# Moving the gates' chain of an mLSTM into the token-major part of a hybrid encoder block, the row product of x later, and neighbourhood operands a head at a time

## The chip, the cores and the metric

The kernel runs on one core of a Trainium2 chip. The core has five engines with queues of their own: TensorE (PE, matmuls and transposes; its weight loads are listed as PEld), VectorE (DVE), ScalarE (ACT), GpSimd (POOL) and SyncE (SP, which here only starts transfers). Each queue is worked off in its order; engines wait for each other by semaphores. The metric is the device time of one execution in microseconds, as the median of several runs.

## The reference

One block of an encoder over 512 tokens of width 1024, in float32. A normalised input is projected once, and three mixers read the projection: a bidirectional mLSTM, a neighbourhood attention on an 8 x 64 grid, and a cross-attention to 256 memory tokens. Cut to what matters here:

```python
h = rms_norm(x, mix_norm_g[l])
proj = h @ w_in[l]      # ml q,k,v,o | ml gates (16) | na q,k,v | xa q | merge gates
# mLSTM, per direction and head, from the gates i_pre, f_pre:
log_f = log_sigmoid(f_pre);  a = cumsum(log_f)
m_new = max(g_c + m, mw_c)                       # a running maximum: a scan
P = exp(D - m_j) * qk;  num = P @ v + inter_w * (C_prev @ q)
# neighbourhood attention, 8 heads of 64:
s = q @ k_band * NA_HEAD_DIM ** -0.5 + bias;  p = softmax(s);  o = p @ v_band
merged = g_ml*(y_ml @ w_br_ml) + g_na*(y_na @ w_br_na) + g_xa*(y_xa @ w_br_xa)
x = x + merged @ w_out
x = x + conv_glu_ffn(rms_norm(x))
return rms_norm(x)
```

## The kernel before, in words

Every big product is float32 accuracy out of three passes: weights and activations are split in a high and a low part, and `mm3` (lines 207 to 209) adds high x high, low x high and high x low in one PSUM bank. Weights come from memory in blocks of 128 x 1024 values or so, three blocks ahead (`emit_raw`, L155, on SP). Each block is split in two halves by `emit_split`: ACT copies the high half (L189, into four rotating buffers `wh`), DVE subtracts to get the low half (L190, `wl`).

The order of the stages on TensorE: four blocks of mLSTM q (`mlq`), four of k (`mlk`), then the *token-major part*, in which tokens lie on the partitions: three groups `c` = 0, 1, 2. Group 0 gives the 16 gates per token and half of the mLSTM's v, group 1 the other half and half of the neighbourhood's v, group 2 the rest. Group `c` is worked in weight blocks `h`; in group 1 there are four blocks of two k tiles, and each block runs over four token tiles `t`, 6 matmuls for each. Then come the other projections (`xaq`, `o`, `memk`, `memv`, `naq`, `nak`), the three branches with their gates (`g` and `br`), the output projection and the feed-forward part.

The attention-like parts are generators, advanced by `step` a few pieces after each block of a projection, so that their small products lie between the large ones. `ml_all` is the mLSTM, `xa_all` the cross-attention, `na_all` the neighbourhood attention; a branch's products wait until its generator is drained. Fewer pieces in one generator let the next start earlier. The code gives the order of emission; a scheduler may still exchange neighbouring instructions on an engine's queue.

What the change touches:

- The normalisation of x as a row (`rstd_row`). POOL raises the mean squares to the power -1/2 (L305); ACT and DVE split the result in two parts (L312, L313); DVE writes eight diagonal 128 x 128 tiles (L318); TensorE multiplies them with ones (L319, two products of 128 x 512) and ACT copies the row `rb` out of PSUM (L321). `proj` calls it inside the second `mlk` block, after k step 0 of 8. All convolutions on q and k (`conv`, L410 to L414, then `silu2`, L419 and L420) need `rb`. Their first instruction empties the PSUM bank that a later block uses again: four banks `mm`, four banks `at`.
- The gates' chain (`ml_prep`, L499 to L588). From the gates `Gt` DVE computes the logarithm of a sigmoid as a series (L503 to L524, with one exponential on ACT, L507) and copies it into `lfc` (L530, L531). Four transposes (L534) turn it into rows; ACT copies them (L536); DVE runs four scans over 512 tokens, two for the running maxima (L540, L541) and two for the sums (L551, L552); ACT copies (L553). DVE subtracts (L558) and POOL stores the result `rd` to memory (L560). Four transposes bring maxima and sums back into columns (L565); ACT takes exponentials and copies (L569, L570). `spread`, hung into the next projection by `late`, sends block sums to all partitions by one product (L573) and computes the decay weights `wt` and `dec` (L575 to L586). `ml_prep` is the first part of `ml_all`, advanced between the blocks of `xaq`.
- After it, per head: SP loads `rd` as rows on all partitions (`load_R`, L600), DVE adds masks (L608), ACT takes exponentials `E` (L660, L664), DVE multiplies them (L665, L667), and TensorE uses them (L675, L677).
- `na_all`. Two heads share 128 partitions. `prep(hp)` writes split operands for both heads of a pair: for each head ACT copies q, k and q again (L759 to L761, 64 x 512) and DVE makes two differences (L762, L763). It runs for the first pair at the start and then after each fourth of the 16 score steps. Each step does scores (L783, L784), a softmax (L788 to L796), transposes a step later (L802, split into `w` at L809, L810) and values two steps later (L821, stored by L833 to L842). The four operand tiles rotate under the tag `R`; bias tiles (L770) rotate under `nab`, a tag that two buffers of the gates' chain share.

Of the kernel before, what the change touches and what calls it, by code (L numbers as in the profile page):

```python
# [11 lines left out]
F32 = mybir.dt.float32  # L12
F32R = mybir.dt.float32r
# [4 lines left out]
P = 128  # L18
# [88 lines left out]
def hybrid_block(ctx, tc, xg, xT, memT, wflat, vecs, gbias, nabias, outa, outb):  # L107
# [14 lines left out]
    def nm(s):  # L122
        uid[0] += 1
        return f"{s}_{uid[0]}"
# [240 lines left out]
    def proj(key, XHs, XLs, n=S, bank=None, at={}):  # L365
        ws = weights(key)
        ps = (bank or mmps)()
        for k in range(KT):
            mm3(ps[:, :n], ws[k][0], ws[k][1], XHs[k], XLs[k], k == 0, k == KT - 1)
            if k == 1:  # L370
                flush()
            if k in at:
                at[k]()
        return ps
# [20 lines left out]

    xsum = two_parts(acc, S)
    ps_k = [proj(("mlk", 0), XH, XL, bank=atps, at={1: lambda: norm.append(rstd_cols(xsum, S, "x"))})]
    ps_k.append(proj(("mlk", 1), XH, XL, bank=atps, at={0: lambda: norm.append(rstd_row(norm[0], S, "x"))}))
    rc, rb = norm
    SY.dma_start(gbf, gbias.partition_broadcast(P))  # L400
    rcc = cp.tile([P, NT], F32, name="rcc")
# [49 lines left out]
    va = va_u.rearrange("p (t h c) -> p t h c", t=4, h=4)  # L451
    G.memset(va[:, :, :, 128:129], C_ML)
    nav_d = dp.tile([S, 1024], F32R, name="nav_d")
    for c in range(3):
        n, nk = TMC[c], TMK[c]
        pss = [(mmps if c % 2 else atps)() for _ in range(NT)]
        for h in range(KT // nk):
            ws = weights(("tm", c, h))
            for t in range(NT):
                tsl = slice(t * P, (t + 1) * P)  # L460
                for k in range(nk):
                    kk = nk * h + k
                    ps = pss[t][:, :n]
                    mm3(ps, XH[kk][:, tsl], XL[kk][:, tsl], ws[k][0], ws[k][1], kk == 0, kk == KT - 1)
        for t in range(NT):
            ps = pss[t]
            if c == 0:
                V.scalar_tensor_tensor(Gt[:, t, :], ps[:, :16], rc[:, t:t + 1], gb, op0=ALU.mult, op1=ALU.add)
            if c < 2:
                o = 16 if c == 0 else 0  # L470
                A.activation(va[:, t, 2 * c:2 * c + 2, 0:128],
                             ps[:, o:o + 256].rearrange("p (h c) -> p h c", h=2), AF.Copy, scale=rcc[:, t:t + 1])
            if c > 0:

                nv = sp.tile([P, 516], F32R, tag="scr", name=nm("nv"))[:, :512]
                nvv = nv.rearrange("p (q y d) -> p q y d", q=2, y=4)
                pv = ps[:, n - 256:n].rearrange("p (q e d) -> p q e d", q=2, e=2)
                A.activation(nvv[:, :, 0:4:3, :], pv, AF.Copy, scale=rc[:, t:t + 1])
                for q in range(2):
                    V.scalar_tensor_tensor(nvv[:, q, 1:3, :], pv[:, q], rc[:, t:t + 1], nvv[:, q, 0:4:3, :].bitcast(F32),  # L480
                                           op0=ALU.mult, op1=ALU.subtract)
                G.dma_start(nav_d[t * P:(t + 1) * P, (c - 1) * 512:c * 512], nv)
    nav_v = nav_d.rearrange("(a r w) f -> a r w f", a=2, r=4)

    def load_vwin(hp):

        vw = unit(F32R)
        for b in range(4):
            for hf in range(2):
                i = 2 * b + hf  # L490
                for r in range(4):
                    G.dma_start(vw[r * 32:(r + 1) * 32, i * 256:(i + 1) * 256],  # L492
                                nav_v[hf, r, CW[b]:CW[b] + 32, hp * 256:(hp + 1) * 256])
        return vw

    ml = {}

# [1 line left out]
    def ml_prep():  # L499
# [54 lines left out]
        yield  # L554
        rr = scr()
        rd = dp.tile([2, 4, S], F32, name="rd")
        yield
        V.tensor_tensor(rr[:36], cu[:36], mr[:36], op=ALU.subtract)  # L558
        for d in range(2):
            G.dma_start(rd[d], rr[32 * d:32 * d + 4, :])  # L560
# [7 lines left out]
        for d, e in ((0, P - 1), (1, 0)):  # L568
            A.activation(T4(cat[:, 32:])[:, :, d, :], pmv[:, :, 32 * d:32 * d + 4], AF.Copy, scale=ident[:, e:e + 1])  # L569
        A.activation(em, pmv[:, :, 0:36], AF.Exp, scale=-1.0)  # L570
        def spread():
            pt = atps()
            PE.matmul(pt[:, :64], ones, cat, start=True, stop=True)  # L573
            both = cp.tile([P, 2, 4, 2, 4], F32, name="both")
            V.tensor_copy(both.rearrange("p a t d h -> p (a t d h)"), pt[:, :64])  # L575
            tot, mh = both[:, 0], both[:, 1]
            V.tensor_tensor(tot, tot, mh, op=ALU.subtract)
            bi = cp.tile([P, 2, 4, 4], F32, name="bi")
            wt = cp.tile([P, 2, 4, 4], F32, name="wt")
            dec = cp.tile([P, 2, 2, 4], F32, name="dec")  # L580
            for d in range(2):
                V.tensor_tensor(bi[:, d], gv[:, :, d, 0, :], pmv[:, :, 64 + 32 * d:68 + 32 * d], op=ALU.subtract)
                V.tensor_tensor(wt[:, d], bi[:, d], tot[:, :, d, :], op=ALU.add)
                V.tensor_tensor(dec[:, d], tot[:, 1:3, d, :], mh[:, 2 * d:2 * d + 2, d, :], op=ALU.add)
            A.activation(wt, wt, AF.Exp)
            st["act"] = A.activation(dec, dec, AF.Exp).ins  # L586
            ml.update(bi=bi, mh=mh, wt=wt, dec=dec)

        ml.update(rd=rd, em=em)
        late.append(spread)  # L590

    def ml_all():
        yield from ml_prep()
        rd, em = ml["rd"], ml["em"]

        def load_R(h):
# [146 lines left out]
    def na_all(nq, nk, vw0, yh, yl):  # L743
# [3 lines left out]
            for e in range(2):  # L747
                G.memset(pair[e][64 - 64 * e:128 - 64 * e].bitcast(F32), 0.0)

        def prep(hp):  # L750
            qn = nq[:, hp * S:(hp + 1) * S]
            kn = nk[:, hp * S:(hp + 1) * S]
            QL = QZ[hp % 2]
            QS, KS = [], []
            for e in range(2):
                own, oth = slice(64 * e, 64 * e + 64), slice(64 - 64 * e, 128 - 64 * e)
                q2 = tp.tile([P, S], F32R, tag="R", name=nm("QS"), bufs=4)
                k2 = tp.tile([P, S], F32R, tag="R", name=nm("KS"), bufs=4)
                A.activation(q2[own], qn[own], AF.Copy)  # L759
                A.activation(k2[own], kn[own], AF.Copy)  # L760
                A.activation(q2[oth], qn[own], AF.Copy)  # L761
                V.tensor_tensor(k2[oth], kn[own], k2[own].bitcast(F32), op=ALU.subtract)  # L762
                V.tensor_tensor(QL[e][own], qn[own], q2[own].bitcast(F32), op=ALU.subtract)  # L763
                QS.append(q2)
                KS.append(k2.rearrange("p (r w) -> p r w", r=ROWS))
            return QS, KS, QL

        def bias_tile(i):
            bt = tp.tile([P, 2 * M], F32, tag="nab", name=nm("nab"))
# [2 lines left out]

        def scores(i, ops, bt):
            QS, KS, QL = ops
            e, bp = (i // 2) % 2, i % 2
            ps = atps()
            sm = scr()
            mx = tiny(2)
            for j in range(2):
                b = 2 * bp + j  # L780
                bs = slice(b * P, (b + 1) * P)
                ks = KS[e][:, :, CW[b]:CW[b] + 32]
                PE.matmul(ps[:, j * M:(j + 1) * M], QS[e][:, bs], ks, start=True, stop=False)  # L783
                PE.matmul(ps[:, j * M:(j + 1) * M], QL[e][:, bs], ks, start=False, stop=True)  # L784
            smv = sm.rearrange("p (a b) -> p a b", a=2)
            for j in range(2):
                js = slice(j * M, (j + 1) * M)
                V.tensor_tensor_reduce(smv[:, j, :], ps[:, js], bt[:, js], 1.0, 2.0 * NEG, ALU.add, ALU.max,  # L788
                                       accum_out=mx[:, j:j + 1])
            V.tensor_scalar(mx, mx, -1.0, None, op0=ALU.mult)  # L790
            su = tiny(2)
            for j in range(2):
                A.activation(smv[:, j, :], smv[:, j, :], AF.Exp, bias=mx[:, j:j + 1], accum_out=su[:, j:j + 1])
            V.reciprocal(su, su)
            for j in range(2):
                A.activation(smv[:, j, :], smv[:, j, :], AF.Copy, scale=su[:, j:j + 1])  # L796
            return sm
# [44 lines left out]
                V.tensor_tensor(ylv[:, b], y4[:, b], yhv[:, b].bitcast(F32), op=ALU.subtract)  # L842

        n = 16
        ops = prep(0)
        bt = bias_tile(0)
        sms, pts = {}, {}
        vws = {0: vw0}
# [1 line left out]
        for t in range(n + 2):  # L850
            if t < n:
                nb = bias_tile(t + 1) if t + 1 < n else None
                sms[t] = scores(t, ops, bt)
                bt = nb
                if t % 4 == 3 and t + 1 < n:
                    ops = prep((t + 1) // 4)
            i = t - 2
            if 0 <= i:
                if i % 4 == 0 and i + 4 < n:
                    vws[i // 4 + 1] = load_vwin(i // 4 + 1)  # L860
                store(i, values(i, pts.pop(i), vws[i // 4]))
            i = t - 1
            if 0 <= i < n:
                pts[i] = transposes(i, sms.pop(i))
            yield
# [503 lines left out]
```

## Time and profile before

| what | value |
|---|---|
| median of 3 runs | 896.11 us (896.08 to 896.44) |
| profiled execution | 896.75 us |
| span of its profile | 895.0 us |
| TensorE busy | 887.5 us (99%) |
| VectorE busy | 584.8 us (65%) |
| ScalarE busy | 452.1 us (51%) |
| granted TensorE clock | 1.000 |
| a 128 x 512 matmul, start to next start in a quiet stretch | 0.23 us |

Times in the trace count from the start of the span. Matmuls overlap: one is recorded as 0.39 us long, but the next starts 0.23 us after it, so a gap on TensorE shows as a larger step between two starts, not as idle time alone. A line of the timeline has the start, the length, the engine, the source line, the operation, the tiles written and read, the shape and the count; in brackets stands how long the engine was idle and who released it. The page's busy line gives time, share of the span and number of instructions for each engine.

### The profile page before, as it was taken

Reading aid. Unit: us, or ns where it says so; the run is one execution under the profiler, and the core shown is the slowest. Engines: PE = TensorE matmul, PEld = TensorE weight load, DVE = VectorE, ACT = ScalarE, POOL = GpSimd, SP = SyncE. Lnnn points to the kernel's source line nnn. Section 1 sums busy time; section 2 is a strip of 40 time slices with the busy share of each in tenths; the row PEclk is TensorE's granted clock in tenths of the full one; section 3 lists DMA queues with packets and bytes.
Section 4 is the critical chain, followed back from the end, with each engine's and each line's share of the span. In section 5 each row is a group of like instructions: output and inputs, shape, how many; then the busy total and the mean of one; then the engine's idle time right before and its main releaser. Section 6 shows DMA issues by size and latency. Waiting matters only on the chain.

```text
span 895.0 us, 12242 instructions
## 1 busy us (share of the span) xinstructions
PE 887.5 (99%) x4332; PEld 739.8 (83%) x4332; DVE 584.8 (65%) x1207; ACT 452.1 (51%) x955; POOL 125.7 (14%) x202
## 2 busy tenths in 40 slices
PE   9999999999999999999999999999999999999997
PEld 7798888988888888888888888888888888888887
DVE  6694587766566757998676558766633466667433
ACT  7363455644555647888644435444422344444432
POOL 0101100000070660420000002111100011111010
PEclk9999999999999999999999999999999999999999
DMA  7223643422242453543323432222233322222412
GB/s 269 78 91 130 196 146 114 169 84 88 89 118 92 102 137 112 146 126 113 118 95 107 141 105 94 95 95 94 74 98 98 108 95 95 96 95 86 139 34 94
DMA packets 39293, 99.68 MB, mean 111 GB/s; under 512 B 5688, under 2 KB 14008, under 8 KB 39232
## 3 DMA queue, kind: packets, MB, share of 16 engines
q1 hardware_dynamic: 31440, 92.32, 30.4%
q0 software_dynamic: 7360, 6.32, 3.4%
q8 instruction: 34, 0.56, 0.3%
q10 hardware_dynamic: 432, 0.26, 0.1%
q14 instruction: 27, 0.22, 0.1%
HBM read 94.67 MB, written 4.21 MB: 110 GB/s over the span
## 4 chain that ended last, share of the span: by engine, by line
PE 96%; ACT 1%; DVE 1%; issue 1%; DMA 1%; POOL 0%; SPq 0%; POOLq 0%; DVEq 0%; ACTq 0%
PE mm L208 28%; PE mm L207 28%; PE mm L209 28%; PE at L208 2%; PE at L209 2%; PE at L207 2%; PE at L821 1%; PE at L675 1%; PE at L802 1%; PE at L640 1%; PE at L677 1%; DMA s<-xT 1%; PE at L909 0%; PE at L784 0%; PE at L783 0%
## 5 line engine op out<-in xcount | busy, mean ns | idle before, releaser
L207 PE MATMUL mm<-u,wh 128*128 128x512 f32 (+1 forms) x1076 | 420.1, 391 | 0.3 <-ACT wh L189 0.3
L208 PE MATMUL mm<-u,wh 128*128 128x512 f32 (+1 forms) x1076 | 418.1, 389 | 0.0
L209 PE MATMUL mm<-u,wl 128*128 128x512 f32 (+1 forms) x1076 | 416.9, 387 | 0.0
L189 ACT ACTIVATE wh<-wr 128x512 fp32r<-128x512 f32 (+3 forms) x299 | 185.4, 622 | 259.0 <-PE mm L208 210.6
L190 DVE TENSOR_TENSOR wl<-wr,wh 128x512 fp32r<-128x512 f32 (+3 forms) x300 | 206.4, 689 | 106.0 <-ACT wh L189 99.9
L207 PEld LDWEIGHTS mm<-u,wh 128*128 128x128 f32 x1076 | 202.4, 188 | 43.5 <-ACT wh L189 0.7
L209 PEld LDWEIGHTS mm<-u,wl 128*128 128x128 f32 x1076 | 202.2, 188 | 43.7 <-DVE wl L190 0.3
L208 PEld LDWEIGHTS mm<-u,wh 128*128 128x128 f32 x1076 | 202.5, 188 | 42.1 <-DVE u L214 0.3
L1238 POOL TENSOR_TENSOR s<-s,rb 128x512 f32<-128x512 f32 x22 | 37.4, 1699 | 255.7 <-DVE s L1237 251.9
L492 POOL DMA_DIRECT2D u<-nav_d x128 | 62.4, 520 | 74.8 <-PE at L821 34.8
L213 ACT ACTIVATE u<-s 128x512 fp32r<-128x512 f32 x26 | 16.4, 631 | 55.7 <-DVE s L1241 55.4
L1241 DVE TENSOR_TENSOR s<-mm,s 128x512 f32<-128x512 f32 x22 | 15.1, 689 | 21.5 <-POOL s L1238 21.5
L412 ACT ACTIVATE s<-pad,vec 128x512 f32<-128x512 f32 x30 | 24.4, 812 | 8.6 <-DVE pad L410 8.6
L413 DVE SCALAR_TENSOR_TENSOR s<-pad,vec,s 128x512 f32<-128x512 f32 x30 | 23.5, 784 | 6.1 <-ACT s L412 6.0
L214 DVE SCALAR_TENSOR_TENSOR u<-s,u 128x512 fp32r<-128x512 f32 x26 | 18.0, 691 | 14.3 <-ACT u L213 14.1
L1237 DVE SCALAR_TENSOR_TENSOR s<-s,s 128x512 f32<-128x512 f32 x22 | 15.2, 692 | 13.4 <-ACT s L1236 13.3
L414 DVE SCALAR_TENSOR_TENSOR s<-pad,vec,s 128x512 f32<-128x512 f32 x30 | 22.5, 749 | 0.8
L1236 ACT ACTIVATE s<-s 128x512 f32<-128x512 f32 x22 | 13.9, 631 | 16.0 <-DVE s L1235 15.9
L305 POOL TENSOR_TENSOR rc<-y,nhalf 128x4 f32<-128x4 f32 x1 | 1.0, 1032 | 147.2 <-DVE y L302 147.2
L410 DVE TENSOR_TENSOR pad<-mm,rb 128x512 f32<-128x512 f32 x22 | 15.1, 690 | 9.7 <-PE mm L209 9.0
L207 PE MATMUL mm<-wh,u 128*128 128x512 f32 x48 | 19.1, 398 | 0.0
L1248 DVE TENSOR_TENSOR u<-mm,u 128x512 f32<-128x512 f32 x13 | 9.0, 691 | 15.3 <-PE mm L209 15.3
(295 smaller groups left out, 1033.9 us busy)
## 6 DMA issues: line engine op xcount, KB each, us to landing
wr<-wflat SPq DMA_DIRECT2D x141, 512.0 KB, 3.2
nab<-nabias SPq DMA_DIRECT2D x16, 256.0 KB, 2.6
u<-nav_d POOLq DMA_DIRECT2D x128, 32.0 KB, 2.6
s<-xT SPq DMA_DIRECT2D x15, 256.0 KB, 3.8
wr<-wflat SPq DMA_DIRECT2D x14, 192.0 KB, 2.3
nav_d<-nv POOLq DMA_DIRECT2D x8, 256.0 KB, 2.4
R<-rd SPq DMA_DIRECT2D x8, 256.0 KB, 3.9
wr<-wflat SPq DMA_DIRECT2D x2, 544.0 KB, 3.2
```

What stands on the lines that cost most here:

```text
L189: A.activation(h[:, u:v], src, AF.Copy)
L190: V.tensor_tensor(l[:, u:v], src, h[:, u:v].bitcast(F32), op=ALU.subtract)
L207: PE.matmul(ps, lh, rh, start=start, stop=False)
L208: PE.matmul(ps, lh, rl, start=False, stop=False)
L209: st["mm"] = PE.matmul(ps, ll, rh, start=False, stop=stop).ins
L213: A.activation(h, src, AF.Copy, scale=scale)
L214: V.scalar_tensor_tensor(l, src, scale, h.bitcast(F32), op0=ALU.mult, op1=ALU.subtract)
L412: A.activation(t1, pad[:, 0:512], AF.Identity, scale=vcol(w, i), bias=vcol(b, i))
L413: V.scalar_tensor_tensor(t1, pad[:, 1:513], vcol(w, n + i), t1, op0=ALU.mult, op1=ALU.add)
L414: V.scalar_tensor_tensor(t1, pad[:, 2:514], vcol(w, 2 * n + i), t1, op0=ALU.mult, op1=ALU.add)
L492: G.dma_start(vw[r * 32:(r + 1) * 32, i * 256:(i + 1) * 256], nav_v[hf, r, CW[b]:CW[b] + 32, hp * 256:(hp + 1) * 256])
L1238: G.tensor_tensor(c, c, rb2, op=ALU.mult)
```

## The change

Three edits.

1. The row product of x is called after k step 3 of the second `mlk` block, not after k step 0.
2. `ml_prep` is no longer part of `ml_all`. It is made a generator of its own before the token-major part, and five pieces of it are advanced inside group 1, after the token tiles listed in `PREP`. One empty piece is dropped, `spread` is called directly and is a piece of its own, and `ml_all` begins at `load_R`. In the new file the lines of `ml_prep` stand about 41 lower: L534 becomes L493, L565 becomes L523, L573 becomes L533; lines in `ml_all` and `na_all` become higher by 6 to 8 (L675 is L683, L821 is L827).
3. `prep` of the neighbourhood attention handles one head. Heads 0 and 1 are prepared at the start, and head `t // 2 + 2` after each second score step.

```diff
-    ps_k.append(proj(("mlk", 1), XH, XL, bank=atps, at={0: lambda: norm.append(rstd_row(norm[0], S, "x"))}))
+    ps_k.append(proj(("mlk", 1), XH, XL, bank=atps, at={3: lambda: norm.append(rstd_row(norm[0], S, "x"))}))
...
         rd = dp.tile([2, 4, S], F32, name="rd")
-        yield
         V.tensor_tensor(rr[:36], cu[:36], mr[:36], op=ALU.subtract)
...
         A.activation(em, pmv[:, :, 0:36], AF.Exp, scale=-1.0)
+        yield
+
         def spread():
...
-        late.append(spread)
+        spread()
+        yield
+
+    prep = ml_prep()
+    PREP = ((0, 0), (0, 2), (1, 3), (2, 1), (2, 3))
     for c in range(3):
...
             for t in range(NT):
...
                     mm3(ps, XH[kk][:, tsl], XL[kk][:, tsl], ws[k][0], ws[k][1], kk == 0, kk == KT - 1)
+                if c == 1 and (h, t) in PREP:
+                    next(prep)
...
     def ml_all():
-        yield from ml_prep()
         rd, em = ml["rd"], ml["em"]
...
-        def prep(hp):
+        def prep(h):
+
+            hp, e = h // 2, h % 2
             qn = nq[:, hp * S:(hp + 1) * S]
             kn = nk[:, hp * S:(hp + 1) * S]
...
-        ops = prep(0)
+        ops = {h: prep(h) for h in range(2)}
...
-                sms[t] = scores(t, ops, bt)
+                sms[t] = scores(t, ops[t // 2], bt)
                 bt = nb
-                if t % 4 == 3 and t + 1 < n:
-                    ops = prep((t + 1) // 4)
+                if t % 2 == 1 and t // 2 + 2 < 8:
+                    ops[t // 2 + 2] = prep(t // 2 + 2)
```

More of the change, by code (lines that the diff above doesn't have):

```diff
@@ L453, in hybrid_block @@
     nav_d = dp.tile([S, 1024], F32R, name="nav_d")
[L454 to L494, printed above, removed]
     ml = {}
@@ L589, in ml_prep, with load_vwin @@
         ml.update(rd=rd, em=em)
-        late.append(spread)
+        spread()
+        yield
+    prep = ml_prep()
+    PREP = ((0, 0), (0, 2), (1, 3), (2, 1), (2, 3))
+    for c in range(3):
+        n, nk = TMC[c], TMK[c]
+        pss = [(mmps if c % 2 else atps)() for _ in range(NT)]
+        for h in range(KT // nk):
+            ws = weights(("tm", c, h))
+            for t in range(NT):
+                tsl = slice(t * P, (t + 1) * P)
+                for k in range(nk):
+                    kk = nk * h + k
+                    ps = pss[t][:, :n]
+                    mm3(ps, XH[kk][:, tsl], XL[kk][:, tsl], ws[k][0], ws[k][1], kk == 0, kk == KT - 1)
+                if c == 1 and (h, t) in PREP:
+                    next(prep)
+        for t in range(NT):
+            ps = pss[t]
+            if c == 0:
+                V.scalar_tensor_tensor(Gt[:, t, :], ps[:, :16], rc[:, t:t + 1], gb, op0=ALU.mult, op1=ALU.add)
+            if c < 2:
+                o = 16 if c == 0 else 0
+                A.activation(va[:, t, 2 * c:2 * c + 2, 0:128],
+                             ps[:, o:o + 256].rearrange("p (h c) -> p h c", h=2), AF.Copy, scale=rcc[:, t:t + 1])
+            if c > 0:
+                nv = sp.tile([P, 516], F32R, tag="scr", name=nm("nv"))[:, :512]
+                nvv = nv.rearrange("p (q y d) -> p q y d", q=2, y=4)
+                pv = ps[:, n - 256:n].rearrange("p (q e d) -> p q e d", q=2, e=2)
+                st["act"] = A.activation(nvv[:, :, 0:4:3, :], pv, AF.Copy, scale=rc[:, t:t + 1]).ins
+                for q in range(2):
+                    V.scalar_tensor_tensor(nvv[:, q, 1:3, :], pv[:, q], rc[:, t:t + 1], nvv[:, q, 0:4:3, :].bitcast(F32),
+                                           op0=ALU.mult, op1=ALU.subtract)
+                G.dma_start(nav_d[t * P:(t + 1) * P, (c - 1) * 512:c * 512], nv)
+    nav_v = nav_d.rearrange("(a r w) f -> a r w f", a=2, r=4)
+    def load_vwin(hp):
+        vw = unit(F32R)
+        for b in range(4):
+            for hf in range(2):
+                i = 2 * b + hf
+                for r in range(4):
+                    G.dma_start(vw[r * 32:(r + 1) * 32, i * 256:(i + 1) * 256],
+                                nav_v[hf, r, CW[b]:CW[b] + 32, hp * 256:(hp + 1) * 256])
+        return vw
     def ml_all():
-        yield from ml_prep()
         rd, em = ml["rd"], ml["em"]
@@ L748, in na_all @@
                 G.memset(pair[e][64 - 64 * e:128 - 64 * e].bitcast(F32), 0.0)
-        def prep(hp):
+        def prep(h):
+            hp, e = h // 2, h % 2
             qn = nq[:, hp * S:(hp + 1) * S]
             kn = nk[:, hp * S:(hp + 1) * S]
[L753 to L766, printed above, removed]
+            ql = QZ[hp % 2][e]
+            own, oth = slice(64 * e, 64 * e + 64), slice(64 - 64 * e, 128 - 64 * e)
+            q2 = tp.tile([P, S], F32R, tag="R", name=nm("QS"), bufs=4)
+            k2 = tp.tile([P, S], F32R, tag="R", name=nm("KS"), bufs=4)
+            A.activation(q2[own], qn[own], AF.Copy)
+            A.activation(k2[own], kn[own], AF.Copy)
+            A.activation(q2[oth], qn[own], AF.Copy)
+            V.tensor_tensor(k2[oth], kn[own], k2[own].bitcast(F32), op=ALU.subtract)
+            V.tensor_tensor(ql[own], qn[own], q2[own].bitcast(F32), op=ALU.subtract)
+            return q2, k2.rearrange("p (r w) -> p r w", r=ROWS), ql
         def bias_tile(i):
@@ L774, in scores @@
             QS, KS, QL = ops
-            e, bp = (i // 2) % 2, i % 2
+            bp = i % 2
             ps = atps()
@@ L781, in scores @@
                 bs = slice(b * P, (b + 1) * P)
-                ks = KS[e][:, :, CW[b]:CW[b] + 32]
-                PE.matmul(ps[:, j * M:(j + 1) * M], QS[e][:, bs], ks, start=True, stop=False)
-                PE.matmul(ps[:, j * M:(j + 1) * M], QL[e][:, bs], ks, start=False, stop=True)
+                ks = KS[:, :, CW[b]:CW[b] + 32]
+                PE.matmul(ps[:, j * M:(j + 1) * M], QS[:, bs], ks, start=True, stop=False)
+                PE.matmul(ps[:, j * M:(j + 1) * M], QL[:, bs], ks, start=False, stop=True)
             smv = sm.rearrange("p (a b) -> p a b", a=2)
```

## The prediction

> **What bounds the kernel now.** I read the page first (busy shares, then the chain), then TensorE's timeline at every place where two matmuls start further apart than their size explains, then the queues of VectorE (DVE) and ScalarE (ACT) around those places.
>
> ```profile
> span 895.0 us, 12242 instructions
> PE 887.5 (99%) x4332; PEld 739.8 (83%) x4332; DVE 584.8 (65%) x1207; ACT 452.1 (51%) x955; POOL 125.7 (14%) x202
> PE 96%; ACT 1%; DVE 1%; issue 1%; DMA 1%; POOL 0%; SPq 0%; POOLq 0%; DVEq 0%; ACTq 0%
> ```
>
> TensorE is busy for 99% of the span and carries 96% of the chain. The timeline in the quiet second half shows the pace: 128x512 matmuls start every 0.231 us.
>
> ```profile
> 600.40 0.39 PE L207 MATMUL mm<-u,wh 128*128 128x512 f32 x1
> 600.63 0.39 PE L208 MATMUL mm<-u,wh 128*128 128x512 f32 x1
> 600.86 0.39 PE L209 MATMUL mm<-u,wl 128*128 128x512 f32 x1
> ```
>
> The change takes no matmul away, so it can only win where starts are further apart than that pace. Three such places lie in its reach. First, the row product of x: two products (L319) wait for the DVE's diagonals.
>
> ```profile
> 34.54 0.39 PE L209 MATMUL at<-u,wl 128*128 128x512 f32 x1
> 35.11 0.47 PE L319 MATMUL at<-s,onesr 128*128 128x512 f32 x1 [0.18 <-DVE s L318]
> 35.81 0.50 PE L319 MATMUL at<-s,onesr 128*128 128x512 f32 x1 [0.22 <-DVE s L318]
> 36.14 0.40 PE L207 MATMUL at<-u,wh 128*128 128x512 f32 x1
> ```
>
> Second, the first use of the mLSTM's decay weights, late because the gates' work came late:
>
> ```profile
> 135.03 0.40 PE L207 MATMUL mm<-u,wh 128*128 128x512 f32 x1
> 135.98 0.71 PE L675 MATMUL at<-u,E 128*128 128x129 f32 x4 [0.55 <-DVE E L665]
> ```
>
> Third, neighbourhood attention; here the worst spot, after both heads' operand copies had gone through ACT in one piece:
>
> ```profile
> 384.40 0.39 PE L207 MATMUL mm<-u,wh 128*128 128x512 f32 x1
> 384.92 0.51 PE L821 MATMUL at<-w,u 128*128 128x256 f32 x2
> ```
>
> And the work that moves, whose length will matter: the four scans on DVE.
>
> ```profile
> 110.17 1.22 DVE L540 TENSOR_TENSOR_SCAN s<-s,at 4x512 f32<-4x512 f32 x1
> 111.40 1.22 DVE L541 TENSOR_TENSOR_SCAN s<-s,at 4x512 f32<-4x512 f32 x1
> 112.63 1.21 DVE L551 TENSOR_TENSOR_SCAN cu<-on,s 4x512 f32<-4x512 f32 x1
> 113.86 1.21 DVE L552 TENSOR_TENSOR_SCAN cu<-on,s 4x512 f32<-4x512 f32 x1
> ```
>
> **The change part by part.** Times are on the clock of the profiled execution; where I name a new place in a queue, it is from the order of the built instructions.
>
> *Row product later.* From the L209 at 34.54 the next product could start at 34.77; the L207 behind the pair starts at 36.14. The pair itself needs 2 x 0.23, so 0.9 us is lost. Three k steps later (nine more matmuls, 2.1 us) TensorE reaches the pair at 36.8, and the last diagonal is written at 35.75: no wait, **-0.9 us**. What is late instead: the row rb, copied at 36.34 to 36.94 now, ends at 38.1. Behind it stand the eight convolutions on DVE (L410 to L420, L410 0.69 us, L413 0.75, L414 0.74), whose first instruction also empties the bank that the third mlk block needs at 40.1: emptied at 38.8, 1.2 us spare. The tightest bank is the third of the first token group, needed at 54.1: I get 53.1. So -0.9 stands; bounds 0 and -0.9.
>
> *Gates' chain, up to the transposes into rows (L534, now L493).* Now the transposes stand at 108.65 and nothing waits. They move to 35 matmuls after the start of the second token group. That start comes at 63.2 (64.10 less 0.9), so TensorE arrives at 63.2 + 35 x 0.232 = 71.3. The chain on DVE (L503 to L530, some 22 small instructions of 0.16 to 0.35 us and one exponential on ACT) ended at 71.17 before. Two things move it: the later rb, and two weight halves (L190, 0.69 us each) that now stand inside it. I followed both queues in the new order with these row durations. The rb delay does not get through: one weight half now runs while rb is awaited, and ACT is held at several points by matmuls that release a weight buffer, and these come 0.9 us earlier; the chain starts 0.3 us earlier than before. The two halves in it cost 0.5 net of what they displaced. It ends at about 71.4, so TensorE waits **+0.15 us**. Bounds: 0; and 2.5 if the whole rb delay (1.2) and both halves (1.4) come on top (71.17 + 2.6 against 71.3). I take my walk, which is near the low end.
>
> *Scans to the transposes back (L565, now L523).* From the first transpose to the moment TensorE may go on: in the rows 108.65 to the end of ACT's copy L553 at 115.79, less 0.3 that DVE spent on a weight half between (109.88 to 110.17), is 6.85 us, of which 4.86 are the scans. Before, 11 us lay between. In the new order 25 matmuls lie between: 4 x 0.11 + 25 x 0.231 = 6.2 us. The copy's end must reach TensorE, 0.05: **+0.65 us**, bounds 0.5 and 0.9 (four scans of equal length leave little room). This is the new cost of the change.
> The Trainium skill, "TensorE: Matmul & The Clock Gate", section "Back-to-back issue gap", gives about 131 ns per matmul for a sustained stream at N=512. By it, as an estimate, the 25 matmuls would cover only 3.7 us, the wait would be 3.2 instead of 0.65, and the sum would be +1.45 instead of -1.1 (897.6). The rows disagree: 0.231 us over thousands of starts, so I give that no chance.
>
> *Chain sums and spread (L573, now L533).* 12 matmuls (2.8 us) after L523; ACT needs 1.1 us (L569 twice, 0.26 each, after the transposes). Hidden. The moved work's own TensorE time (0.44 + 0.35 + 0.13) only changes place.
>
> *What the moved work passes.* On DVE two weight halves of the fourth block of this group stand behind the scans: done at about 79, needed at 81.3. On POOL the two rd stores (0.53 us each) now precede the eight nav_d stores; nobody waits for these until 340. On SP the loads of R and the first two bias tiles (which wait for the scans' buffers, about 79) now precede weight loads needed after 91: landing 3.2 us. No cost; if SP stood 8 us longer it would show on ACT.
>
> *First decay weights (L675, now L683).* E then waits neither for the gates nor, on DVE, for the second head's weighting (two L625 of 0.56) ahead of it. Its last input is now an eviction of 0.69 and a product of 0.42 behind the block before; I get E ready 0.1 us before TensorE asks. **-0.6** of the 0.7; bounds 0 and -0.7.
>
> *Neighbourhood operands.* Per head three copies on ACT (0.63, 0.61, 0.63) and two on DVE (0.69): same number. Before, two heads went at once in a step, one step before their use, between 376.9 and 382.7; TensorE lost 0.7 us between 380 and 385, and 0.4 more at two or three other crowded steps. After, one head goes every other step, two steps ahead of its use; the copies now stand between the scores and the split weights (L815) that the values need. After the second scores TensorE has 24 matmuls and 4 transposes, 6.0 us; ACT has 4.2 us and DVE 4.9 us of queue until the second half is split. **-0.4**; bounds -1.1 and +3.5 (see the rivals).
>
> Sum: -0.9 + 0.15 + 0.65 - 0.6 - 0.4 = **-1.1 us**. The profiled execution took 896.75 us (span 895.0 and 1.75 around it), 0.64 above the median of 896.11. So 896.75 - 1.1 = 895.65, and against the median 895.0, 0.12% faster. A measurement of this kernel can tell about 0.2% (1.8 us) from no change.
>
> **The rivals.**
> *All cover holds:* the chain is in time, and the neighbourhood's 1.1 and L675's 0.7 vanish: -0.9 + 0.65 - 0.7 - 1.1 = -2.05, 894.1. For it: every spot is short of its cover by tenths. Against: 0.65 stays, and some crowded steps remain in the new order.
> *The gates hold TensorE at L493:* 2.5 instead of 0.15, 897.4. It decides against the change from 1.25 us of wait on. For it: the convolutions fill DVE from 37 to 66 with few gaps. Against: the early pace is set by ACT's buffer waits.
> The same page, section "Why this matters for your kernels", wants no gap above about 3 us, or the clock halves; this trace has a granted clock of 1.00 throughout and no wait above 0.7, and 2.5 would stay below.
> *Copies in front of the split weights (ends slower):* each of the six later heads' copies costs what the one crowded place cost, 0.7. Then 6 x 0.7 - 0.7 = +3.5 instead of -0.4: +2.8, 898.9. It ends slower by 0.2% from 0.53 us a head on. Against: no such loss shows at the later double steps, and the copies are now due a step later.
> *The early win is handed back:* rb late by 1.2 leaves a bank full when the token groups want it, 0.9 lost: 895.9. The change would then not do what its first part says.
>
> **How the numbers follow.** Forecast 0.56, with its own range 894.2 to 896.3; all cover holds 0.16; gates late 0.13; copies 0.09; win handed back 0.06. Faster than 894.3: most of the second case and the first's tail, 0.17. Slower than 897.9: the copies and a tail of the gates, 0.12. Within: 0.71. The range reaches from just under the second case to beyond the third, 893.9 to 897.9.
>
> **What would show it.** L319 back to back with the matmuls around it near 36.8; a wait of a few tenths at L493 near 71; 0.5 to 0.9 before L523 near 78; none above 0.2 at the first L683; in the neighbourhood stage L827 waits below 0.3 each. I am wrong if L493 waits over 1 us, if L523 does not wait, or if the copies L767 to L769 stand before waits of L827.

## The result and the profile after

The changed kernel takes 897.34 us (median of 22 runs, 897.04 to 898.34), the kernel before 896.15 us beside it (22 runs). The ratio is 1.0015, with a 95% interval of 1.0009 to 1.0022: the change costs 1.2 us, where the prediction had a gain of 1.1 us. The profiled execution took 897.34 us, with a span of 895.6 us. Its page:

```profile
span 895.6 us, 12235 instructions
PE 887.3 (99%) x4332; PEld 739.0 (83%) x4332; DVE 582.9 (65%) x1207; ACT 452.6 (51%) x955; POOL 126.0 (14%) x202
...
PE 93%; DVE 3%; ACT 1%; issue 1%; DMA 0%; SPq 0%; POOLq 0%; POOL 0%; ACTq 0%; DVEq 0%
```

The busy times are the same to 0.4%; less of the chain lies on TensorE (93%, was 96%) and more on DVE (3%, was 1%). TensorE now waits for DVE somewhere. To find where, I took from the trace, for each pair of successive starts on TensorE, the step less the pace of that shape (0.231 us for 512 columns, 0.118 for 256, and so on), and added these up by stretches. The first 20 us are left out of all that follows: they hold waits for the first weights, which lie between 1.4 and 2.2 us in the profiled executions of these kernels, and the change touches nothing there.

| stretch, us | before | after | what is there |
|---|---|---|---|
| 20 to 40 | 0.88 | -0.08 | the row product, L319 |
| 40 to 60 | -0.10 | -0.09 | mlk, start of the token-major part |
| 60 to 80 | 0.01 | 1.60 | second token group: L493 and L523 |
| 80 to 120 | -0.02 | 0.21 | third group, xaq |
| 120 to 180 | 1.22 | 0.91 | first heads of the mLSTM |
| 180 to 340 | 0.52 | 0.27 | the rest of it, cross-attention |
| 340 to 440 | 2.00 | 2.15 | neighbourhood |
| 440 to 520 | -0.31 | 0.39 | last branch, output projection |
| 520 to the end | 0.31 | 0.33 | feed-forward part |
| sum | 4.52 | 5.68 | |

The sums differ by 1.16 us, which is the 1.2 us of the medians. Three stretches carry most of it: 0.96 us gained at the row product, 1.59 lost between 60 and 80 us, and 0.70 lost between 440 and 520 us. Of the rest, gains of 0.31 at the first decay weights and 0.25 behind them stand against losses of 0.23 and 0.15. Only the first went as forecast. In TensorE's timeline of the changed kernel, the row product stands back to back with its neighbours, and both gates' transposes now wait:

```profile
36.25 0.63 PE L319 MATMUL at<-s,onesr 128*128 128x512 f32 x2
36.72 0.39 PE L207 MATMUL at<-u,wh 128*128 128x512 f32 x1
...
70.47 0.40 PE L208 MATMUL mm<-wl,u 128*128 128x512 f32 x1
71.33 0.62 PE L493 MATMUL at<-ident,lfc 128*100 128x128 f32 x4 [0.46 <-DVE lfc L489]
...
77.34 0.40 PE L209 MATMUL mm<-wh,u 128*128 128x512 f32 x1
78.35 0.56 PE L523 MATMUL at<-ident,s 100*128 100x100 f32 x4 [0.62 <-ACT s L512]
```

The steps at L493 and L523 are 0.86 and 1.01 us; less the 0.231 of a matmul, 0.63 and 0.78 are lost. The other 0.19 us of the stretch lies in many steps that are a few hundredths or thousandths longer: the first of the four transposes takes 0.125 and 0.143 us to the next, 0.108 and 0.088 in a kernel where neither place waits. A third wait is in the neighbourhood stage, at transposes, where none was forecast:

```profile
360.28 0.40 PE L208 MATMUL mm<-u,wh 128*128 128x512 f32 x1
361.31 0.84 PE L808 MATMUL at<-ident,s 128*128 128x128 f32 x4 [0.64 <-ACT s L802]
```

0.80 us is lost in this one step. The stretch as a whole lost only 0.15 more than before, because other steps of it lose less: 0.3 us from 380 to 385 us, where the kernel before lost 0.7. The loss between 440 and 520 us shows in no single step: from 460 us on every matmul takes some 2 or 3 ns longer.

### The profile page after: what moved, and what is told of

The parts are those of the page before. It is cut to its first block, busy times and chain, and to the rows that moved or that the text cites. A ratio compares the mean times of both kernels' runs of the same rounds, so it can differ in the third digit from the quotient of the medians.

```text
span 895.6 us, 12235 instructions
## 1 busy us (share of the span) xinstructions
PE 887.3 (99%) x4332; PEld 739.0 (83%) x4332; DVE 582.9 (65%) x1207; ACT 452.6 (51%) x955; POOL 126.0 (14%) x202
## 4 chain that ended last, share of the span: by engine, by line
PE 93%; DVE 3%; ACT 1%; issue 1%; DMA 0%; SPq 0%; POOLq 0%; POOL 0%; ACTq 0%; DVEq 0%
PE mm L207 28%; PE mm L208 28%; PE mm L209 28%; PE at L208 1%; PE at L209 1%; PE at L207 1%; PE at L827 1%; PE at L683 1%; PE at L808 1%; PE at L648 1%; DVE wl L190 1%; PE at L685 1%; DMA wr<-wflat 0%; PE at L664 0%; PE at L915 0%
## 5 line engine op out<-in xcount | busy, mean ns | idle before, releaser
L1039 DVE TENSOR_TENSOR s<-mm,rb_x 128x512 f32<-128x512 f32 x16 | 11.0, 688 | 13.2 <-PE mm L209 13.1
```

## The experiments

All of them compute the whole of the reference. Times stand beside runs of the kernel before on the same chip; the sums of steps are made as in the table above, against 4.52 us for before and 5.68 for the changed kernel.

**The parts alone.** First, each of the three edits on the kernel before, and the whole change with the gates' pieces further apart.

```diff
 # row product alone, on the kernel before
-... at={0: lambda: norm.append(rstd_row(norm[0], S, "x"))}))
+... at={3: lambda: norm.append(rstd_row(norm[0], S, "x"))}))
```

> Kernel before, with the row product of x alone moved from k step 0 to k step 3. Theory (the difference is the sum of the places at which TensorE's starts lie apart): the two L319 stand at the pace of 0.23 us, the 0.34 + 0.46 + 0.2 us beside them go, nothing else changes: -0.9 us, no wait at L493's or L808's relatives that before did not have. Rival (the win is handed back): the later row leaves PSUM banks full and 0.5 to 0.9 us of new steps shows between 40 and 65 us: 0 to -0.4 us.

Measured: 895.14 us against 895.81, ratio 0.9991 (0.9982 to 1.0000). The stretch from 20 to 40 us goes from 0.88 to -0.08, and nothing shows between 40 and 80 us. The first edit is worth 0.96 us by the steps and is not handed back there; the medians differ by 0.7 us, with an interval from 0 to 1.6.

```diff
 # gates' chain alone: the changed kernel with
-... at={3: lambda: norm.append(rstd_row(norm[0], S, "x"))}))
+... at={0: lambda: norm.append(rstd_row(norm[0], S, "x"))}))
 # and prep(hp), scores(), values' loop of na_all as before
```

> Kernel before, with the gates' chain alone moved into the second token group; row product and neighbourhood as before. Theory A (the wait at L493 is the chain's own length against 35 matmuls): 0.4 to 0.7 us at L493, 0.65 to 0.8 at L523, the 0.71 at the first decay weights gone with some 0.2 at L648 in its place: +0.7 to +1.0 us in all. Theory B (the wait at L493 comes from the row of x being copied 1.2 us later, behind which DVE's convolutions are late): below 0.2 us at L493, 0.65 to 0.8 at L523: +0.2 to +0.5 us. Either way 340 to 440 us stays as before; if it does not, the moved chain changes the neighbourhood stage too.

Measured: 897.48 us against 895.81, ratio 1.0018 (1.0009 to 1.0027); the sum of steps is 5.87. L493 waits 0.72 us and L523 does not wait, and the 0.80 us near 360 us and the slower pace from 460 to 520 us are there in full, without the edit to the neighbourhood. So the gates' chain alone makes the kernel slower: of the 1.35 us that the sum grows by, 0.80 are lost where the chain runs, and the rest in stages far behind it.

Neither theory on L493 was right as I wrote it. The scheduler put L493 after 28 matmuls of the group here, after 35 in the changed kernel, so the waits can't be compared as they are; the chain can. VectorE's timeline of this kernel, from the chain's first instruction to its last:

```profile
66.13 0.17 DVE L462 COPY y<-Gt 128x32 f32<-128x32 f32 x1
...
69.81 0.68 DVE L190 TENSOR_TENSOR wl<-wr,wh 128x512 fp32r<-128x512 f32 x1
70.42 0.24 DVE L489 COPY lfc<-cat 128x16 f32<-128x16 f32 x2
```

And of the changed kernel, in which the row product comes later:

```profile
65.12 0.18 DVE L462 COPY y<-Gt 128x32 f32<-128x32 f32 x1
65.20 0.69 DVE L190 TENSOR_TENSOR wl<-wr,wh 128x512 fp32r<-128x512 f32 x1
65.80 0.69 DVE L420 SCALAR_TENSOR_TENSOR u<-s,s 128x512 f32<-128x512 f32 x1
...
68.73 0.68 DVE L190 TENSOR_TENSOR wl<-wr,wh 128x512 fp32r<-128x512 f32 x1
...
69.43 0.68 DVE L190 TENSOR_TENSOR wl<-wr,wh 128x512 fp32r<-128x512 f32 x1
...
70.93 0.25 DVE L489 COPY lfc<-cat 128x16 f32<-128x16 f32 x2
```

With the row as before, the chain runs for 4.5 us with one weight half in it, as it did in the kernel before. With the row later it begins 1.0 us earlier (TensorE is 1.0 us earlier, the group starts at 62.57 instead of 63.58) but has three weight halves and the last convolution's L420 in it and ends 0.5 us later. Counted from the start of the group it needs 7.1 us in the one and 8.6 in the other. 35 matmuls cover 8.1: they would have hidden the first, and they don't hide the second. The later row is what fills the queue: the last L420 ends 2.6 us after the start of the group in the one (at 66.21) and 3.9 us after it in the other (at 66.49).

```diff
 # neighbourhood operands alone, on the kernel before
-        ops = prep(0)
+        ops = {h: prep(h) for h in range(2)}
...
-                if t % 4 == 3 and t + 1 < n:
-                    ops = prep((t + 1) // 4)
+                if t % 2 == 1 and t // 2 + 2 < 8:
+                    ops[t // 2 + 2] = prep(t // 2 + 2)
```

> Kernel before, with the neighbourhood operands alone prepared a head at a time. Theory A (the copies of one head on ACT stand in front of the softmax scale L796 of a step): 0.6 to 0.9 us at the first transposes (L802 in before) near 360 us, the 0.3 at 384 gone: +0.1 to +0.7 us. Theory B (what was lost there comes from the changed phase of the stages ahead, not from the copies): no step above 0.2 us near 360, -0.4 us as predicted.

Measured: 896.54 us against 895.81, ratio 1.0006 (0.9997 to 1.0015), not told from no change; the sum of steps is 4.60, and the stretch of the neighbourhood has 2.05, before 2.00. Theory A falls: nothing is lost near 360 us. Theory B had the place right and the gain wrong: the 0.29 us near 384 us is still there. The prediction took the copies of two heads in one piece for its cause; with those of one head it is the same. The third edit is worth nothing.

```diff
 # gates' pieces further apart, on the changed kernel
-    PREP = ((0, 0), (0, 2), (1, 3), (2, 1), (2, 3))
+    PREP = ((0, 0), (1, 2), (2, 1), (3, 0), (3, 2))
```

> The changed kernel with the five pieces of the gates' chain further apart: L493 after 42 matmuls of the group, not 35, and L523 36 matmuls behind it, not 25. Theory (cover alone decides): 0.63 and 0.78 us go, so 1.4 us below the changed kernel, 0.2 us below before. Rival (the chain holds DVE and the weight halves of the group's last block come late): the 25 and 36 matmuls are covered, but 0.3 to 1 us shows at the first matmul of that block, near 79 us.

Measured: 896.23 us against 895.81, ratio 1.0005 (0.9996 to 1.0013); the sum of steps is 4.17, 1.5 below the changed kernel. The stretch from 60 to 80 us has 0.00 us: both waits are gone, and none shows at the group's last block. The rival falls. The time did not go below that of before, although I had expected it to; the interval (0.4 us faster to 1.2 slower) holds the expected 0.2 us of gain too. 360 us and 460 to 520 us still lose what they lose in the changed kernel.

**The phase.** What the gates' move does to stages 300 us later can't be its work, which is done by 85 us (L546 at 84.29). But the mLSTM's generator is four pieces shorter without it, and each block of a projection advances a fixed number of pieces. Everything behind it then runs four pieces earlier and meets other blocks. Near 360 us, in VectorE's timeline of the changed kernel, the softmax of the step that waits stands between the output evictions of two branch blocks (L1063, L1064) and behind a weight half:

```profile
356.04 0.67 DVE L1063 SCALAR_TENSOR_TENSOR s<-s,mm 128x512 f32<-128x512 f32 x1
...
356.98 0.68 DVE L1064 TENSOR_TENSOR u<-u,s 128x512 f32<-128x512 f32 x1
...
358.49 0.17 DVE L796 TENSOR_SCALAR y<-y 128x2 f32<-128x2 f32 x1
...
359.60 0.69 DVE L190 TENSOR_TENSOR wl<-wr,wh 128x512 fp32r<-128x512 f32 x1
360.21 0.16 DVE L800 RECIPROCAL y<-y 128x2 f32<-128x2 f32 x1
```

The kernel before, for a step of the same kind, where L790 and L794 are these two instructions:

```profile
357.02 0.17 DVE L790 TENSOR_SCALAR y<-y 128x2 f32<-128x2 f32 x1
...
358.62 0.15 DVE L794 RECIPROCAL y<-y 128x2 f32<-128x2 f32 x1
```

The scores of that step start at 354.10 before and at 355.13 after; the reciprocal comes 4.5 and 5.1 us behind them. To test the phase by itself, I put four empty pieces where the chain had been.

```diff
 # on the changed kernel
     def ml_all():
+        for _ in range(4):
+            yield
         rd, em = ml["rd"], ml["em"]
```

> The changed kernel with four empty pieces at the start of the mLSTM's generator, as many as the gates' chain had there, so that every later stage meets the same blocks of the projections as before; the chain itself stays in the second token group, L493 and L523 unchanged. Theory (phase: the mLSTM's generator is four pieces shorter, so cross-attention and neighbourhood run four pieces earlier, and their steps fall on other blocks and other buffers): the 0.80 us before the transposes near 360 us goes back to below 0.2, 440 to 520 us goes back to the pace of before (0.7 us), the 0.63 and 0.78 at L493 and L523 stay: about 0.9 to 1.4 us below the changed kernel. Rival (the chain in its new place delays the neighbourhood by its loads or buffers): 360 and 440 to 520 us stay as changed, 0 us.

Measured: 896.14 us against 895.97, ratio 1.0001 (0.9992 to 1.0010), so 1.2 us below the changed kernel's median (1.0 when each is set against the runs of before beside it); the sum of steps is 4.32. The transposes near 360 us no longer wait. In TensorE's timeline of this kernel:

```profile
358.47 0.39 PE L207 MATMUL mm<-u,wh 128*128 128x512 f32 x1
358.82 0.44 PE L810 MATMUL at<-ident,s 128*128 128x128 f32 x2
```

The stretch from 440 to 520 us is back at -0.31, and that from 120 to 180 us falls to 0.33: with the old phase the first decay weights gain 0.89 us, not the 0.31 of the changed kernel. Their first product (L685 here) follows the matmul before it without a wait:

```profile
135.27 0.40 PE L207 MATMUL mm<-u,wh 128*128 128x512 f32 x1
135.50 0.61 PE L685 MATMUL at<-u,E 128*128 128x129 f32 x4
```

In the changed kernel it does not wait either, but two later products of that stretch (L648, at 138.8 and 168.7 us) lose 0.24 and 0.22. L493 and L523 still lose 0.62 and 0.79. This is the theory's case; the rival falls.

```diff
 # both: four empty pieces, and the gates' pieces further apart
+        for _ in range(4):
+            yield
...
-    PREP = ((0, 0), (0, 2), (1, 3), (2, 1), (2, 3))
+    PREP = ((0, 0), (1, 2), (2, 1), (3, 0), (3, 2))
```

> The same with the chain's pieces further apart, as in the spaced experiment. If both causes are right and independent, both gains add: 1.4 from L493 and L523, 0.9 to 1.4 from the phase, so 2.3 to 2.8 us below the changed kernel and 1.1 to 1.6 us below before: some 894.4 to 894.9 where before has 895.9. If the early chain costs something that neither place shows, it stays at or above the kernel with the row product alone moved (895.1).

Measured: 894.76 us against 895.97, ratio 0.9984 (0.9975 to 0.9993); the sum of steps is 2.94. In TensorE's timeline the transposes have no bracket, and nobody waits:

```profile
72.50 0.60 PE L493 MATMUL at<-ident,lfc 128*100 128x128 f32 x4
...
81.20 0.51 PE L523 MATMUL at<-ident,s 100*128 100x100 f32 x4
```

The two causes are independent and add up, 2.6 us below the changed kernel by the medians, of 2.3 to 2.8 expected.

```diff
 # the same, with prep(hp), scores() and the loop of na_all as before
```

> As the one before, with the neighbourhood operands prepared for two heads at once, as in the kernel before. Theory (a head at a time is worth nothing with this phase, as the experiment with that part alone showed): the same time within 0.3 us, the 0.3 us step near 383 us in both. Rival: 0.4 us more than the one before.

Measured: 894.32 us against 895.97, ratio 0.9982 (0.9973 to 0.9991); the sum of steps is 2.67, and the neighbourhood has 1.94 against 2.17 with a head at a time. The medians differ by 0.4 us, less than the 0.8 by which each interval reaches to either side. A head at a time is worth nothing, and costs perhaps 0.2 us: with the old phase the neighbourhood loses 1.8 to 2.0 us in the kernels with pairs and 2.05 to 2.17 in those with a head at a time. This kernel is the best of all that ran: 1.65 us below before (0.8 to 2.4) and 3.0 below the change as made. Its span and chain on the page:

```profile
span 892.4 us, 12239 instructions
...
PE 98%; ACT 1%; issue 0%; DVE 0%; POOLq 0%; POOL 0%; DVEq 0%
```

**The slower pace.** The activations that stream through TensorE in the output projection lie in large buffers that many stages share, and with the other phase the buffers are handed out in another order. The built programs show it: the 192 matmuls of the output projection read these activations at one set of addresses in the kernel before and all kernels with its phase, and at another in the changed kernel and those with its phase; their weights and PSUM banks lie in the same places in all. A kernel with two empty pieces gives a third phase and a third set of places.

```diff
-        for _ in range(4):
+        for _ in range(2):
```

> The changed kernel with two empty pieces, not four: neither the phase of before nor that of the change, and the large buffers of the last stages lie in other places than in either. If the phase decides, the neighbourhood shows a third pattern of steps between 340 and 440 us. For the slower pace between 460 and 520 us (0.2332 us a matmul changed, 0.2301 before): theory (the places of the buffers set it) some value other than these two or one of them by chance; rival (what decides is the chain's new place ahead of it) 0.233 again.

Measured in one run: 898.18 us, sum of steps 6.29. A third pattern indeed: 1.01 us at transposes of the mLSTM's output (L711, 239.6 us) that lose nothing in any other kernel, 0.56 and 0.57 at L810 near 362 and 388 us, and a mean step of 0.2311 us in the output projection, neither 0.2302 nor 0.2333. The rival, that the chain's new place sets the pace, falls.

The last two runs change only the places of these activations: high and low part of a tile in one buffer, the same four buffers, the same instructions in the same order.

```diff
-    GH = [mhu[k // 4][:, (k % 4) * S:(k % 4 + 1) * S] for k in range(KT)]
-    GL = [mhu[2 + k // 4][:, (k % 4) * S:(k % 4 + 1) * S] for k in range(KT)]
+    GH = [mhu[k // 2][:, (k % 2) * S:(k % 2 + 1) * S] for k in range(KT)]
+    GL = [mhu[k // 2][:, (2 + k % 2) * S:(3 + k % 2) * S] for k in range(KT)]
```

> The changed kernel, with the split merged activations of the output projection laid out differently in the same four buffers: high and low part of a k tile lie in one buffer, not in two. Instructions, their order and their number stay; only addresses that some 190 matmuls of the output projection read (between about 475 and 520 us) differ. Theory (the places of the operands set the pace there): their mean step moves from 0.2333 us by at least 0.0005. Rival (the pace is a state that comes from earlier in the program, or from the clock): 0.2333 again. The matmuls ahead of the output projection (460 to 475 us) keep 0.231 to 0.232 either way.

> The same other layout in the kernel with spaced gates, four empty pieces and operands in pairs, where the output projection runs at 0.2301 us a matmul. Theory (places): a mean step other than 0.2301 by at least 0.0005, either way, so up to 0.6 us in the time. Rival (a state from earlier): 0.2301 again and the time of the kernel it is made from, 894.3.

The same 191 steps of the output projection, between the same two matmuls in TensorE's timeline, first in the changed kernel:

```profile
475.17 0.39 PE L208 MATMUL mm<-u,wh 128*128 128x512 f32 x1
...
519.74 0.39 PE L207 MATMUL mm<-u,wh 128*128 128x512 f32 x1
```

With four empty pieces (places as before):

```profile
474.64 0.39 PE L208 MATMUL mm<-u,wh 128*128 128x512 f32 x1
...
518.60 0.40 PE L207 MATMUL mm<-u,wh 128*128 128x512 f32 x1
```

The changed kernel with the other layout:

```profile
475.33 0.39 PE L208 MATMUL mm<-u,wh 128*128 128x512 f32 x1
...
519.78 0.40 PE L207 MATMUL mm<-u,wh 128*128 128x512 f32 x1
```

44.57, 43.96 and 44.45 us for 191 steps, so 0.2333, 0.2302 and 0.2327 us a step (the 0.2301 of the expectations is a mean over part of them). In the best kernel the other layout moves it from 0.2302 to 0.2320. The theory holds in both: the places of the operands alone change the pace. With the other layout it stays nearer to that of the changed kernel (0.0006 us away) than to that of before, so which part of a place matters is not shown. The times agree as far as they can: 897.45 us in one run of the changed kernel, and 895.28 us against 896.01 for the other, ratio 0.9994 (0.9985 to 1.0003), where its sum of steps is 0.5 above that of the kernel it was made from. Which places are good, and why, stays open: I tried three sets and one other layout in two of them, and found no rule.

## Why the prediction was wrong, point by point

- *Row product later* (-0.9): right, -0.96. The pair stands at 36.25, not 36.8, because the first 20 us of the profiled execution were 0.6 us shorter; the row is copied as late as I had worked out.
- *Gates' chain at L493* (+0.15): the sign was right, the size wrong, 0.63. The step that failed is my walk of DVE's queue. I let the chain start 0.3 us earlier and lengthened it by 0.5; it started 1.0 earlier and took 1.5 longer. I had counted two weight halves more, but not that the last convolution's L420 would also come to lie inside. "The rb delay does not get through" was false: with the row as before, the chain ended 7.1 us after the start of the group, with the later row 8.6. The bound of 2.5 held; the rival "the gates hold TensorE at L493" was nearer than I thought, without reaching its 1.25 us.
- *Scans to L523* (+0.65): 0.78, within its bounds of 0.5 and 0.9. Counting matmuls against the rows of the scans worked; the terms as I wrote them, 6.85 + 0.05 - 6.2, make 0.70, not 0.65. The Trainium skill, "TensorE: Matmul & The Clock Gate", section "Back-to-back issue gap", with its 131 ns would have had 3.2 us here, as an estimate; the trace, with 0.78 us and a step of 0.231, does not agree with it.
- Beside the two waits that stretch lost 0.19 us in many steps slightly longer than the pace, which the prediction had at nothing. Its sum for 60 to 80 us was 0.80 and it is 1.60.
- *First decay weights* (-0.6): -0.31 in the changed kernel. The first product no longer waits, as I had read from E's inputs, and with the old phase the whole gain is there (-0.89); the new phase took two thirds back. One line of the change that the diff ahead of the prediction does not show bears on it too: the first `E` are queued on ACT behind the last eviction of the token-major part (L582, `st["act"]`), no longer behind the exponential of `dec`. No experiment takes that line alone.
- *Neighbourhood operands* (-0.4): nothing, or 0.2 us of loss. The spot near 384 us, my worst one, loses 0.28 to 0.32 us in every kernel with the old phase, with pairs and with a head at a time alike, so the copies were not what it waited for. The waits at L827 did stay below 0.3, as I wrote, and the copies L767 to L769 stand before no wait of L827. But I had priced only the order of instructions inside a step. The one large wait, 0.80 us, came at the transposes, and not from this edit: it is there without it, and gone with the old phase.
- *The step that failed most: what the moved work passes ("No cost").* I followed the moved instructions past each queue, but not what their removal does to the generator that they leave. The text before the prediction even says that fewer pieces in one generator let the next start earlier. I put the cost of that at nothing. With the old phase the kernel loses 1.36 us less (sums 5.68 and 4.32): 0.70 by the places of the buffers between 440 and 520 us, 0.58 between 120 and 180 us, 0.17 between 80 and 120 us and 0.09 in the neighbourhood, less 0.21 that the stretch from 180 to 340 us gains by it.
- *The sum.* The forecast of -1.1 us and the 1.16 of the table lie 2.3 us apart: 0.8 from L493, L523 and the steps beside them, 0.3 from the first decay weights, 0.55 from the neighbourhood and 0.7 from the pace between 440 and 520 us; the other stretches cancel.
- *The range* (893.9 to 897.9) held the time, at its far end and by other mechanisms than the rivals named, so that was luck. None of the three signs by which I would have been wrong came (L493 over 1 us, no wait at L523, copies before waits of L827). No rival was "later stages meet other blocks", and that was the largest single term.

## What to carry to other kernels

When work is advanced in pieces against the blocks of something else, moving a piece out shifts every later stage; put an empty piece in its place, and the move can be judged and priced by itself. A chain moved under cover has to be measured in matmuls from the point at which its input is ready, with everything that its engine's queue holds in between; 0.6 and 0.8 us of cover too little at two places cost 1.6 us here. Before a change is given up, its parts are worth trying apart: the idea of this one was sound, and with its cover and phase mended and its third edit left out it is 0.18% faster, not 0.15% slower.

## What the runs showed of the hardware

The pace of a 128 x 512 matmul depends on where its streaming operand, here the activations, lies in SBUF, the on-chip memory. With the same instructions in the same order, the output projection ran at a mean step of 0.2302, 0.2311, 0.2320, 0.2327 or 0.2333 us, and each set of places gave its value again to 0.1 ns in every kernel that had it: 0.2302 in six kernels, 0.2333 in three, the kernel before and the changed one among them. Single steps lie between 0.225 and 0.241 us in a pattern that repeats. The granted clock of that stretch was 1.00 in all of them. The Trainium skill, "SBUF — State Buffer", section "Who interferes with whom", gives TensorE two read ports of its own, one for the moving operand and one for weights, and names only the pair that VectorE shares with GpSimd as a place of contention. That section says nothing of addresses; here they mattered, by up to 1.4%. Over the 3210 matmuls of this size that `mm3` puts into the `mm` banks 1.4% would be 10 us, as an estimate from these steps and a bound that nothing here shows can be reached.
